# Gate and up projections in seven products of 256 tokens instead of eight

## The chip, the cores and the metric

The kernel runs on one core of a Trainium2 chip. The metric is the device time of one execution in microseconds (us). The median of three runs before the change is 852.94 us, and the three lie between 852.77 and 853.24 us. Names of the engines in the profile: PE is TensorE's matmul, PEld its weight load, DVE is VectorE, ACT is ScalarE, POOL is GpSimd, SP is SyncE, whose queue starts nearly all transfers.

## The reference

A decoder layer on 512 tokens of width 1024, all in float32:

```
proj = x @ w_in                            # q, k, v, SSM input, gate logits
y_attn = merged(dilated attention) @ w_attn_br
y_ssm  = glu(S5 scan) @ w_ssm_br
mix_out = (g0 * y_attn + g1 * y_ssm) @ w_out
h  = layer_norm(ALPHA * x + mix_out)
ff = (silu(h @ w_ff_gate) * (h @ w_ff_up)) @ w_ff_down     # 1024 -> 2816 -> 1024
x  = layer_norm(ALPHA * h + ff)
```

The change touches the last but one line alone: the products of `h` with `w_ff_gate` and `w_ff_up` (1024 by 2816 each, 22 column tiles of 128).

## The kernel before, in words

Every large product is made of three matmuls. An operand in float32 is split into a rounded part `hi` (type fp32r) and the rest `lo`, and `mm3` (lines 187 to 190) adds hi·hi, hi·lo and lo·hi into the same PSUM columns. The helper `split` (lines 179 to 185) makes the two parts: ACT copies `hi` (line 181), DVE subtracts to get `lo` (line 182).

`class Weights` streams the weights. `load` starts a transfer of one unit of 128 x 2048 floats (1 MB) on SP into one of two `raw` buffers; `split` turns half a unit (128 x 1024) into a pair `whi`, `wlo` in one of five slots (three in the early part); `release`, called in the program after the matmuls that used a slot, hands the oldest slot back and splits the next half unit. Since the order of instructions on each engine is the order in which the program issues them, these calls set the order of the work; there is no planner.

The feed-forward stage begins after the first layer norm. `turn_h` (lines 1137 to 1145) transposes 128 tokens of `h` on PE and splits the result into `hp_` (`hh`, `hl` in the profile: channels on partitions, 512 tokens along the free axis, two tiles of four 128-channel blocks each). `ff_mm(f, e, cs)` multiplies column tile `f` of the gate (`e` = 0) or up (`e` = 1) weights with the tokens `cs`: eight blocks of 128 channels, three matmuls each, 24 matmuls into one PSUM bank (`fg` in the profile). The weights are the stationary operand, the tokens stream. The first tiles run on 256 tokens at a time while the other tokens are still being transposed (lines 1202 to 1211), all others on 512. `ff_gate(f)` (lines 1187 to 1200) forms gate times sigmoid times up from the two banks with one ACT tanh and two DVE operations, and splits the result at once into `ff` hi and lo.

The down projection follows (lines 1228 to 1274): `down` uses the tokens of `ff` as the stationary operand and 512 columns of `w_ff_down` as the streaming one, into eight banks (`dn`), k-tile by k-tile. The last four k-tiles go token tile by token tile, so that the second layer norm of one token tile lies beside the matmuls of the next. `hn` holds the first layer norm's result for the residual all this time.

SBUF is managed by hand: `home(n, ...)` gives one of about a dozen 128 x 2048 areas a new name once its former content is dead, and the pool `ap_` has four more (`act`).

## Time and profile before

| what | value |
|---|---|
| median of three runs | 852.94 us |
| span of the profiled execution, first to last instruction | 851.2 us (the profile gives no other time for it; what lies around the span is 852.94 - 851.2 = 1.7 us against the median) |
| granted TensorE clock, mean | 0.998 |
| PE / PEld / DVE / ACT busy | 842.6 / 701.9 / 485.3 / 302.5 us |
| gate and up matmuls (`fg`) | 144 of 256 columns, 984 of 512 columns |
| feed-forward stage on PE | first `fg` matmul at 481.93 us, first `dn` matmul at 724.00 us |
| weight splits, all stages | 134 on ACT (1046 ns each), 134 on DVE (1227 ns each) |

Matmuls are pipelined: a matmul's listed duration contains its way through the array, and the next one starts long before it ends. Their pace is read from the distance of their starts.

### The profile page before, as it was taken

The page shows a single profiled execution, that of the slowest core. Times are in us where ns is not written, and L with a number is a line of the kernel's source. Part 1 is how long each engine was busy: PE and PEld are TensorE (multiplying, and loading weights), DVE is VectorE, ACT ScalarE, POOL GpSimd, SP SyncE. Part 2 cuts the span into 40 slices and gives each one's busy share as a digit, 9 for nine tenths or more (in the row PEclk, how much of TensorE's full clock was granted, in tenths as well). Part 3 has the DMA queues.
Part 4 walks back from the last instruction along what each step waited for, and adds up shares of the span by engine and source line. Part 5 has one row for each costly group of instructions (what it writes and reads, how often), then busy time and mean ns, then how long its engine had stood idle before and what let it go on. Part 6 is the DMA issues. An engine that isn't in the chain of part 4 may idle for free.

```text
span 851.2 us, 11299 instructions
## 1 busy us (share of the span) xinstructions
PE 842.6 (99%) x4576; PEld 701.9 (82%) x4576; DVE 485.3 (57%) x951; ACT 302.5 (36%) x481; POOL 25.5 (3%) x27
## 2 busy tenths in 40 slices
PE   9999999999999999999999999999999999999996
PEld 7888888888888888888888898888888888888886
DVE  6976899964666446347785854334344344222237
ACT  5973231264344444643241332222222222211101
POOL 0000000000000000000000500000000000000005
PEclk9999999999999999999999999999999999999999
DMA  9732421425121221121642142222222222322203
GB/s 332 185 120 89 124 99 53 146 73 176 50 99 50 102 98 52 50 91 58 248 142 105 50 149 99 99 99 99 99 100 98 89 90 88 136 98 95 99 0 100
DMA packets 23860, 90.06 MB, mean 106 GB/s; under 512 B 6272, under 2 KB 11136, under 8 KB 14464
## 3 DMA queue, kind: packets, MB, share of 16 engines
q1 hardware_dynamic: 22032, 86.59, 29.8%
q10 hardware_dynamic: 1776, 2.74, 0.9%
q8 instruction: 36, 0.59, 0.3%
q14 instruction: 16, 0.13, 0.0%
HBM read 84.87 MB, written 4.46 MB: 105 GB/s over the span
## 4 chain that ended last, share of the span: by engine, by line
PE 98%; DMA 1%; DVE 0%; ACT 0%; issue 0%; SPq 0%; DVEq 0%
PE fg L190 9%; PE fg L188 9%; PE fg L189 9%; PE dn L190 4%; PE dn L189 4%; PE dn L188 4%; PE pg L188 4%; PE pg L189 3%; PE pg L190 3%; PE pv L188 3%; PE pk L188 3%; PE pq L188 3%; PE pv L189 3%; PE pq L190 3%; PE pv L190 3%; PE pk L189 3%
## 5 line engine op out<-in xcount | busy, mean ns | idle before, releaser
L182 DVE TENSOR_TENSOR wlo<-raw,whi 128x1024 fp32r<-128x1024 f32 x134 | 164.2, 1227 | 191.3 <-ACT whi L181 191.2
L181 ACT CAST whi<-raw 128x1024 fp32r<-128x1024 f32 x134 | 140.0, 1046 | 232.8 <-PE dn L190 73.3
L188 PE MATMUL fg<-hh,whi 128*128 128x512 f32 (+1 forms) x376 | 141.3, 376 | 0.0
L189 PE MATMUL fg<-hl,whi 128*128 128x512 f32 (+1 forms) x376 | 141.2, 375 | 0.0
L190 PE MATMUL fg<-hh,wlo 128*128 128x512 f32 (+1 forms) x376 | 141.2, 375 | 0.0
L189 PEld LDWEIGHTS fg<-hl,whi 128*128 128x128 f32 x376 | 70.8, 188 | 12.9
L190 PEld LDWEIGHTS fg<-hh,wlo 128*128 128x128 f32 x376 | 70.8, 188 | 12.8
L188 PEld LDWEIGHTS fg<-hh,whi 128*128 128x128 f32 x376 | 70.8, 188 | 12.7
L188 PE MATMUL dn<-whi,ff 128*128 128x512 f32 x168 | 65.4, 389 | 0.0
L189 PE MATMUL dn<-wlo,ff 128*128 128x512 f32 x168 | 65.4, 389 | 0.0
L190 PE MATMUL dn<-whi,ff 128*128 128x512 f32 x168 | 65.4, 389 | 0.0
L188 PE MATMUL pg<-x_hi,whi 128*128 128x512 f32 x128 | 50.5, 395 | 0.0
L184 ACT ACTIVATE ff<-fth 128x512 fp32r<-128x512 f32 x22 | 14.0, 635 | 102.7 <-DVE fth L322 102.7
L190 PE MATMUL pg<-x_hi,wlo 128*128 128x512 f32 x128 | 49.9, 390 | 0.0
L189 PE MATMUL pg<-x_lo,whi 128*128 128x512 f32 x128 | 49.9, 390 | 0.0
L322 DVE TENSOR_TENSOR fth<-fth,fg 128x512 f32<-128x512 f32 x22 | 15.1, 687 | 56.9 <-PE fg L190 56.8
L188 PE MATMUL pq<-x_hi,whi 128*128 128x512 f32 x96 | 37.9, 394 | 0.0
L188 PE MATMUL pk<-x_hi,whi 128*128 128x512 f32 x96 | 37.8, 394 | 0.0
L190 PE MATMUL pq<-x_hi,wlo 128*128 128x512 f32 x96 | 37.4, 390 | 0.0
L190 PE MATMUL pk<-x_hi,wlo 128*128 128x512 f32 x96 | 37.4, 389 | 0.0
L189 PE MATMUL pk<-x_lo,whi 128*128 128x512 f32 x96 | 37.4, 389 | 0.0
L189 PE MATMUL pq<-x_lo,whi 128*128 128x512 f32 x96 | 37.4, 389 | 0.0
(257 smaller groups left out, 1458.4 us busy)
## 6 DMA issues: line engine op xcount, KB each, us to landing
raw<-in_w_in SPq DMA_DIRECT2D x26, 1024.0 KB, 4.8
raw<-in_w_gu SPq DMA_DIRECT2D x22, 1024.0 KB, 4.7
raw<-in_w_dn SPq DMA_DIRECT2D x11, 1024.0 KB, 4.7
raw<-in_w_br SPq DMA_DIRECT2D x4, 1024.0 KB, 4.7
raw<-in_w_out SPq DMA_DIRECT2D x4, 1024.0 KB, 4.7
raw_x<-in_xw SPq DMA_DIRECT2D x2, 1024.0 KB, 9.9
raw<-in_w_glu SPq DMA_DIRECT2D x2, 1024.0 KB, 4.8
xn<-in_x SPq DMA_DIRECT2D x2, 1024.0 KB, 8.0
```

The costliest lines, as they stand in the source:

```text
L181: act.copy(hi, src)
L182: dve.tensor_tensor(lo, src, hi.bitcast(F32), op=ALU.subtract)
L184: act.mul(hi, src, scale)
L188: pe.matmul(dst, a[0], b[0], start=first, stop=False)
L189: pe.matmul(dst, a[0], b[1], start=False, stop=False)
L190: pe.matmul(dst, a[1], b[0], start=False, stop=last)
L322: eng.tensor_tensor(o, a, b, op=op)
```

## The change

Column tiles 0 and 1 stay as they are (`NPLAIN` = 2). The other 20 tiles are taken in ten pairs. For a pair, the weights are seen as four blocks: a11 and a12 are tile 2j (gate and up) with the first and the last four channel blocks, a21 and a22 the same of tile 2j+1; `h` is four blocks too, by channel half and by token half. Strassen's scheme (with Winograd's sums) then needs seven products of blocks where the plain way needs eight. One product is 24 matmuls of 256 columns: two column tiles (gate, up), four channel blocks, three matmuls.

- **Sums of `h`**, once: four DVE operations of 128 x 1024 on a float32 copy `ht` of the transposed `h`, then three splits (`t23` of 2048 columns, `t4` and `t1` of 1024). `turn_h` writes that copy with one more ACT operation per 512 columns.
- **Sums of weights**, for each pair: four DVE operations of 128 x 1024 into `sums`. A pair has seven split operands (three plain blocks, four sums) where it had four. A split's DVE half (`lo`) is put off to the next call of `flush`.
- **Products** for pair j in the order 2, 5, 6, 3, 7, (1 of the next pair), 4, with three banks per pair, which alternate. Bank x takes 1, 6, 7, 4 one upon the other, bank z takes 5 and 3, bank y takes 2. Between two products into one bank its state is read out (`evict`): ACT copies 1, 5, 6 and 4; DVE adds in after 2, 3 and 7. After product 4 ACT makes one tanh of 1024 columns, and DVE finishes the pair with two operations of 1024 columns (`finish_pair`), placed ahead of the read-out of the next product 2.
- **ff** is kept in float32 and split in the down stage (`ff_split`, 11 times 128 x 1024), two of these already beside the last products.
- **hn** is written to DRAM in four transfers (0.5 MB each) at the start of the stage, since its areas take `ff`, and is read back in two (1 MB each) at the start of the down stage.

The weights' bytes are the same; their layout in DRAM is prepared on the host so that each half unit is one block.

```diff
 N_BR = N_GLU + 4
 N_OUT = N_BR + 8
 N_FF = N_OUT + 8
-N_DOWN = N_FF + 2 * NFF
+NPLAIN = 2
+N_DOWN = N_FF + 2 * NPLAIN
 NLAST = 4
 
...
+        if self.first_loads and 2 * m == self.first_job:
+            self.first_loads.popleft()()
             return
...
+        if self.jobs and n == self.first_job:
+            self.jobs.popleft()()
+            return
+        self.flush()
...
+    def flush(self):
+        if self.after:
+            self.after()
+            self.after = None
...
-    for f in range(NFF):
+    for f in range(NPLAIN):
         w.add(i["w_gu"][f], 8)
+    w.first_job = 2 * len(w.units)
...
+    NPR = NFF // 2
+    ra, rb = {}, {}
+
+    def load_a(j):
+        if j < NPR:
+            ra[j] = wp.tile([P, 2048], F32, tag="wraw", name=f"ra{j}", bufs=2)
+            sp.dma_start(ra[j], i["w_gu"][2 * j])
+        else:
+            w.load()
+
+    def load_b(j):
+        if j < NPR:
+            rb[j] = home(("g0", 2)[j % 2], f"rb{j}")
+            sp.dma_start(rb[j], i["w_gu"][2 * j + 1])
+
+    w.first_loads.extend((lambda j=j: load_a(j)) for j in (1, 2))
...
-            split(hp_[0][j][:, :, tsl], hp_[1][j][:, :, tsl], b.rearrange("p (e c) -> p e c", e=4))
+            bv = b.rearrange("p (e c) -> p e c", e=4)
+            full = ht[t // 2][:, 4 * j : 4 * j + 4, 128 * (t % 2) : 128 * (t % 2) + 128]
+            act.copy(full, bv)
+            act.copy(hp_[0][j][:, :, tsl], bv)
+            tt(hp_[1][j][:, :, tsl], full, hp_[0][j][:, :, tsl].bitcast(F32), ALU.subtract)
...
+    FF_HOMES = ("act", "g2", 0, "g3", 4, 5)
+    ffs = {}
+
+    def ff_at(f, n):
+        if f // 4 not in ffs:
+            h = FF_HOMES[f // 4]
+            z = ap_.tile([P, 2048], F32, tag="act", name=f"ff{f // 4}") if h == "act" else home(h, f"ff{f // 4}")
+            ffs[f // 4] = z.rearrange("p (f t) -> p f t", f=4)
+        return ffs[f // 4][:, f % 4 : f % 4 + n, :]
...
-        tt(th, th, fb[f, 1], ALU.mult)
-        split(cur[:, 0, f % 2, :], cur[:, 1, f % 2, :], th, 0.5)
+        tt(ff_at(f, 1)[:, 0, :], th, fb[f, 1], ALU.mult)
...
+    sums = home(6, "sums").rearrange("p (n c) -> p n c", n=2)
+    quad = home(3, "quad").rearrange("p (c e t) -> p c e t", c=4, e=2)
+    ops = {}
+    for j in (1, 2):
+        load_b(j)
+
+    def prepare(j, n):
+        hi, lo = w.take_slot(f"{j}{n}")
+        ops[j, n] = tuple(z.rearrange("p (e k c) -> p e k c", e=2, k=4) for z in (hi, lo))
+        a11, a12 = (ra[j][:, 1024 * e : 1024 * e + 1024] for e in range(2))
+        a21, a22 = (rb[j][:, 1024 * e : 1024 * e + 1024] for e in range(2))
+        s0, s1 = sums[:, 0], sums[:, 1]
+        src = {1: a11, 2: a12, 4: a22, 5: s0, 6: s1, 3: s0, 7: s1}[n]
+        if n == 5:
+            tt(s0, a21, a22, ALU.add)
+        elif n == 6:
+            tt(s1, s0, a11, ALU.subtract)
+        elif n == 3:
+            tt(s0, a12, s1, ALU.subtract)
+        elif n == 7:
+            tt(s1, a11, a21, ALU.subtract)
+        act.copy(hi, src)
+        w.flush()
+
+        def rest():
+            tt(lo, src, hi.bitcast(F32), ALU.subtract)
+            if n == 7:
+                load_a(j + 2)
+            elif n == 4:
+                load_b(j + 2)
+
+        w.after = rest
+
+    order = [(1, 1)]
+    for j in range(1, NPR):
+        order += [(j, 2), (j, 5), (j, 6), (j, 3), (j, 7)] + [(j + 1, 1)] * (j + 1 < NPR) + [(j, 4)]
+    w.jobs.extend((lambda j=j, n=n: prepare(j, n)) for j, n in order)
+
+    psb = {}
+
+    def product(j, n):
+        x, y, z = ((4, 5, 6), (1, 0, 7))[(j - 1) % 2]
+        b = {1: x, 2: y, 5: z}.get(n)
+        key = {1: "x", 6: "x", 7: "x", 4: "x", 2: "y", 5: "z", 3: "z"}[n]
+        if b is not None:
+            psb[j, key] = bank(b, f"fs{j}{key}")
+        d = psb[j, key]
+        wh, wl = ops.pop((j, n))
+        mh, ml = forms[n]
+        for e in range(2):
+            for k in range(4):
+                c = d[:, 256 * e : 256 * e + 256]
+                for m, (p_, q_) in enumerate(((wh, mh), (wh, ml), (wl, mh))):
+                    pe.matmul(c, p_[:, e, k, :], q_[:, k, :], start=(b is not None and e == k == m == 0),
+                              stop=(k == 3 and m == 2), skip_group_check=True)
+
+    snap = {}
+
+    def taken(name, j):
+        snap[name] = bt.tile([P, 512], F32, tag=f"snap{name}", name=f"snap{name}{j}", bufs=1)
+        return snap[name]
+
+    def quarter(c):
+        return quad[:, c].rearrange("p e t -> p (e t)")
+
+    def finish_pair(j):
+        th, gate, up = snap["th"], quad[:, :, 0, :], quad[:, :, 1, :]
+        stt(th, th, 1.0, gate, ALU.add, ALU.mult)
+        tt(ff_at(2 * j, 2).rearrange("p f (h t) -> p (f h) t", h=2), th, up, ALU.mult)
+
+    def evict(j, n):
+        if n == 1:
+            act.copy(taken("1", j), psb[j, "x"])
+        elif n == 2:
+            if j > 1:
+                finish_pair(j - 1)
+            tt(quarter(0), snap["1"], psb[j, "y"], ALU.add)
+        elif n == 5:
+            act.copy(taken("5", j), psb[j, "z"])
+        elif n == 6:
+            act.copy(taken("6", j), psb[j, "x"])
+        elif n == 3:
+            tt(quarter(1), snap["6"], psb[j, "z"], ALU.add)
+        elif n == 7:
+            tt(quarter(3), snap["5"], psb[j, "x"], ALU.add)
+        else:
+            act.copy(quarter(2), psb[j, "x"])
+            snap["th"] = bt.tile([P, 1024], F32, tag="fth", name=f"fth{j}s", bufs=1).rearrange("p (c t) -> p c t", c=4)
+            act.activation(snap["th"], quad[:, :, 0, :], AF.Tanh, scale=0.5)
...
+    for t in range(NTT):
+        sp.dma_start(hdr[:, t, :], hn[t])
+
+
+    h1, h2 = ht
+    tt(h1[:, 0:4], h2[:, 0:4], h1[:, 0:4], ALU.subtract)
+    tt(h2[:, 0:4], h2[:, 4:8], h2[:, 0:4], ALU.subtract)
+    tt(h2[:, 4:8], h2[:, 4:8], h1[:, 0:4], ALU.subtract)
+    tt(h1[:, 4:8], h1[:, 4:8], h2[:, 4:8], ALU.subtract)
+    t23 = [ap_.tile([P, KT, 256], F32R, tag="act", name=f"t23{n}") for n in "hl"]
+    t4 = ap_.tile([P, 2, 4, 256], F32R, tag="act", name="t4")
+    t1 = [hp_[n][0][:, :, 256:512] for n in range(2)]
+    forms = {1: [hp_[n][0][:, :, 0:256] for n in range(2)], 2: [hp_[n][1][:, :, 0:256] for n in range(2)],
+             3: [hp_[n][1][:, :, 256:512] for n in range(2)], 4: [t4[:, n] for n in range(2)], 5: t1,
+             6: [t23[n][:, 4:8] for n in range(2)], 7: [t23[n][:, 0:4] for n in range(2)]}
...
+        if n == 0:
+            split(t23[0], t23[1], h2)
+        elif n == 1:
+            split(t4[:, 0], t4[:, 1], h1[:, 4:8])
...
-    for f in range(2, NFF):
-        for e in range(2):
-            ff_mm(f, e, slice(0, 512))
-            w.release()
-        ff_gate(f)
...
+    split(t1[0], t1[1], h1[:, 0:4])
+
+    ffhl = {}
+    SPLIT_HOMES = ((7, "g1"), (8, 1), ("act", "act"), ("act", 6), ("act", "g2"), (0, "g3"))
...
+        fs = slice(2 * (jj % 2), 2 * (jj % 2) + 2)
+        split(ffhl[s_][0][:, fs, :], ffhl[s_][1][:, fs, :], ffs[s_][:, fs, :], 0.5)
+
+    for j, n in order:
+        product(j, n)
+        evict(j, n)
+        w.release()
+        if j == NPR - 1 and n in (3, 7):
+            ff_split((0, 1)[n == 7])
...
+    finish_pair(NPR - 1)
+
+    hns = []
+    for j, h in enumerate(("g0", 2)):
+        hns.append(home(h, f"hr{j}").rearrange("p (t d) -> p t d", t=2))
+        sp.dma_start(hns[j], hdr[:, 2 * j : 2 * j + 2, :])
...
+        if k % 2 == 0:
+            ff_split(k // 2 + 2)
...
+    gu = pairs(gu, 8, P).reshape(NFF, P, 2, 2, 512)
+    gu = np.concatenate([gu[:NPLAIN], gu[NPLAIN:].transpose(0, 1, 3, 2, 4)]).reshape(NFF, P, 2048)
```

Three places of the order, each before and after. The line numbers after the change are those of the changed kernel.

PE where one group of 24 matmuls ends and the next begins (`fg`, `fs` are PSUM banks; `hh`, `hl`, `t23h`, `t23l` operands from `h`). Before, within the plain tiles:

```order
L188 MATMUL fg_4813<-hh_3888,whi_91_4705 128x512
L189 MATMUL fg_4813<-hl_3890,whi_91_4705 128x512
L190 MATMUL fg_4813<-hh_3888,wlo_91_4706 128x512
L188 MATMUL fg_4850<-hh_3887,whi_92_4742 128x512 [waits Activation_49]
L189 MATMUL fg_4850<-hl_3889,whi_92_4742 128x512
L190 MATMUL fg_4850<-hh_3887,wlo_92_4743 128x512 [waits DVE_49]
```

After, from product 5 to product 6 of pair 3 (bank z to bank x):

```order
L1296 MATMUL fs3z<-hh_3887,whi_35_4881 128x256
L1296 MATMUL fs3z<-hl_3889,whi_35_4881 128x256
L1296 MATMUL fs3z<-hh_3887,wlo_35_4882 128x256
L1296 MATMUL fs3x<-t23h,whi_36_4913 128x256 [waits Activation_49]
L1296 MATMUL fs3x<-t23l,whi_36_4913 128x256
L1296 MATMUL fs3x<-t23h,wlo_36_4914 128x256 [waits DVE_49]
```

The groups still have 24 matmuls and wait at their start for the two halves of a split; the matmuls have 256 columns, and the group writes into a bank that holds an earlier product.

DVE over one pair of column tiles in the middle of the stage (`wlo` is the second half of a split, `fth` and `ff` the gating). Before, the whole of it:

```order
L182 TENSOR_TENSOR wlo_102_5076<-raw_4975,whi_102_5075 128x1024 [waits DMAHW5_49,Activation_49]
L182 TENSOR_TENSOR wlo_103_5105<-raw_4975,whi_103_5104 128x1024 [waits PE_49,Activation_49]
L319 SCALAR_TENSOR_TENSOR fth_5110<-fth_5110,fg_5050 128x512 [waits Activation_49]
L322 TENSOR_TENSOR fth_5110<-fth_5110,fg_5079 128x512 [waits DVE_49,PE_49]
L185 SCALAR_TENSOR_TENSOR ff_5043<-fth_5110,ff_5043 128x512 [waits Activation_49]
L182 TENSOR_TENSOR wlo_104_5142<-raw_5041,whi_104_5141 128x1024 [waits DMAHW6_49,Activation_49]
L182 TENSOR_TENSOR wlo_105_5171<-raw_5041,whi_105_5170 128x1024 [waits PE_49,Activation_49]
L319 SCALAR_TENSOR_TENSOR fth_5177<-fth_5177,fg_5116 128x512 [waits Activation_49]
L322 TENSOR_TENSOR fth_5177<-fth_5177,fg_5145 128x512 [waits DVE_49,PE_49]
L185 SCALAR_TENSOR_TENSOR ff_5176<-fth_5177,ff_5176 128x512 [waits Activation_49]
```

After, 12 of the 16 rows of a pair: `sums` are weight sums, `quad` the read-outs with a sum, `fth2s` the end of the pair before:

```order
L337 TENSOR_TENSOR sums<-rb_4633 128x1024 [waits DMAHW3_49,DVE_49]
L337 TENSOR_TENSOR wlo_32_4851<-ra_4572,whi_32_4850 128x1024 [waits Activation_49]
L337 TENSOR_TENSOR sums<-sums,ra_4572 128x1024 [waits DVE_49]
L337 TENSOR_TENSOR wlo_35_4882<-sums,whi_35_4881 128x1024 [waits Activation_49]
L337 TENSOR_TENSOR sums<-ra_4572,sums 128x1024 [waits DVE_49]
L337 TENSOR_TENSOR wlo_36_4914<-sums,whi_36_4913 128x1024 [waits Activation_49]
L334 SCALAR_TENSOR_TENSOR fth2s<-fth2s,quad 128x1024 [waits Activation_49]
L337 TENSOR_TENSOR ff_4976<-fth2s,quad 128x1024 [waits DVE_49]
L337 TENSOR_TENSOR quad<-snap_4911,fs3y 128x512 [waits DVE_49,PE_49]
L337 TENSOR_TENSOR sums<-ra_4572,rb_4633 128x1024
L337 TENSOR_TENSOR wlo_33_4946<-sums,whi_33_4945 128x1024 [waits Activation_49]
L337 TENSOR_TENSOR wlo_37_4980<-sums,whi_37_4979 128x1024 [waits Activation_49]
```

The pair had ten DVE operations and has 16, 13 of them of 1024 columns. The weight sums stand ahead of the subtractions that need them, and the end of pair 2 stands between the sums of pair 3.

ACT over the same stretch (`whi` is the first half of a split). Before, for two column tiles:

```order
L181 CAST whi_88_4609<-raw_4509 128x1024 [waits DMAHW6_49,PE_49]
L181 CAST whi_89_4638<-raw_4509 128x1024 [waits PE_49,Activation_49]
L1197 ACTIVATE fth_4645<-fg_4584 128x512 [waits PE_49,Activation_49]
L184 ACTIVATE ff_4644<-fth_4645 128x512 [waits DVE_49]
L181 CAST whi_90_4676<-raw_4576 128x1024 [waits DMAHW7_49,PE_49]
L181 CAST whi_91_4705<-raw_4576 128x1024 [waits PE_49,Activation_49]
L1197 ACTIVATE fth_4711<-fg_4651 128x512 [waits PE_49,Activation_49]
L184 ACTIVATE ff_4644<-fth_4711 128x512 [waits DVE_49]
```

After, all 12 rows of a pair (`snap` are read-outs without a sum, `quad<-fs2x` that of product 4):

```order
L1264 CAST whi_35_4881<-sums 128x1024 [waits DVE_49,PE_49,Activation_49]
L1315 COPY snap_4911<-fs3x 128x512 [waits PE_49]
L1264 CAST whi_36_4913<-sums 128x1024 [waits DVE_49,Activation_49]
L1329 COPY quad<-fs2x 128x512 [waits PE_49]
L1331 ACTIVATE fth2s<-quad 128x1024 [waits Activation_49]
L1264 CAST whi_33_4945<-sums 128x1024 [waits DVE_49]
L1264 CAST whi_37_4979<-sums 128x1024 [waits DVE_49]
L1321 COPY snap_5009<-fs3z 128x512 [waits PE_49]
L1264 CAST whi_41_5011<-ra_4793 128x1024 [waits DMAHW4_49]
L1323 COPY snap_5041<-fs3x 128x512 [waits PE_49]
L1264 CAST whi_34_5043<-rb_4633 128x1024 [waits DMAHW3_49]
L1264 CAST whi_42_5072<-ra_4793 128x1024
```

Each read-out now stands between two copies for the splits, and copies that take a weight sum wait for DVE.

33 lines of the change are left out of this document (18 added, 15 removed).

## The prediction

> **What bounds the kernel now.** I read the page first (busy times, then the chain of waits), then the groups by shape, then the start times on PE. The page's head, its busy row and the engines in its chain:
>
> ```profile
> span 851.2 us, 11299 instructions
> PE 842.6 (99%) x4576; PEld 701.9 (82%) x4576; DVE 485.3 (57%) x951; ACT 302.5 (36%) x481; POOL 25.5 (3%) x27
> PE 98%; DMA 1%; DVE 0%; ACT 0%; issue 0%; SPq 0%; DVEq 0%
> ```
>
> PE is busy for 99% of the span and makes 98% of the chain. Whatever shortens PE's stream shortens the kernel, as long as DVE (57%) and ACT (36%) keep up. The groups by shape that this change touches (mean ns of one after the comma):
>
> ```profile
> L188 PE MATMUL fg<-hh,whi 128*128 128x512 f32 x328 | 127.6, 389 | 0.0
> L188 PE MATMUL fg<-hh,whi 128*128 128x256 f32 x48 | 13.7, 284 | 0.0
> L182 DVE TENSOR_TENSOR wlo<-raw,whi 128x1024 fp32r<-128x1024 f32 x134 | 164.2, 1227 | 191.3 <-ACT whi L181 191.2
> L181 ACT CAST whi<-raw 128x1024 fp32r<-128x1024 f32 x134 | 140.0, 1046 | 232.8 <-PE dn L190 73.3
> L322 DVE TENSOR_TENSOR fth<-fth,fg 128x512 f32<-128x512 f32 x22 | 15.1, 687 | 56.9 <-PE fg L190 56.8
> L1197 ACT ACTIVATE fth<-fg 128x512 f32<-128x512 f32 x22 | 13.0, 593 | 0.0
> L764 ACT COPY v<-pv 128x512 f32<-128x512 f32 x12 | 7.1, 589 | 7.5 <-PE pv L190 7.2
> ```
>
> A matmul's listed time (389 ns for 512 columns, 284 for 256) holds its way through the array. The pace is the distance of starts, from the timeline of PE:
>
> ```profile
> 489.55 0.28 PE L189 MATMUL fg<-hl,whi 128*128 128x256 f32 x1
> ...
> 500.82 0.28 PE L190 MATMUL fg<-hh,wlo 128*128 128x256 f32 x1
> 500.94 0.40 PE L188 MATMUL fg<-hh,whi 128*128 128x512 f32 x1
> ...
> 723.78 0.39 PE L190 MATMUL fg<-hh,wlo 128*128 128x512 f32 x1
> 724.00 0.39 PE L188 MATMUL dn<-whi,ff 128*128 128x512 f32 x1
> ```
>
> From 489.55 to 500.82 us 94 matmuls of 256 columns start after one another: 11.27 / 94 = 0.1199 us. From 500.94 to 723.78 us it is 983 of 512 columns (984 = 3 x 328, less the first): 222.84 / 983 = 0.2267 us. So half the columns cost 53%, not 50%: about 13 ns of each matmul do not scale. The pace is not idle time in disguise, and it holds beside busy neighbours, as the windows say (columns: length, then busy time and count of PE, PEld, DVE, ACT, POOL, granted clock):
>
> ```profile
> 484.50:487.50 3.00, 3.00 (x27) 3.00 (x27) 3.00 (x4) 0.00 (x0) 1.81 (x2) 1.00 0.00 0
> 489.60:500.80 11.20, 11.20 (x95) 11.20 (x95) 6.34 (x10) 4.84 (x7) 0.00 (x0) 1.00 0.46 154
> 502.00:724.00 222.00, 222.00 (x981) 183.81 (x980) 90.37 (x102) 63.07 (x82) 0.00 (x0) 1.00 0.28 98
> 724.00:835.00 111.00, 111.00 (x491) 91.93 (x490) 32.58 (x38) 20.31 (x20) 3.64 (x4) 1.00 0.24 82
> ```
>
> In the first window DVE is busy all the time, and 27 matmuls (some two of them cut by its edges) still take 3.00 us. In the 256-column stretch the weight load is busy all the time as well (11.20 of 11.20), against 184 of 222 us among the 512-column ones.
>
> **The PE term.** A pair of column tiles had 2 x 2 x 24 = 96 matmuls of 512 columns, 96 x 0.2267 = 21.76 us. It gets 7 x 24 = 168 of 256 columns, 168 x 0.1199 = 20.14 us; one product is 2.88 us. Ten pairs: 217.6 - 201.4 = 16.2 us saved. Seven eighths of the arithmetic would have been 27.2 us; the 13 ns on 720 more matmuls take the rest. The point of no gain is a pace of 960 x 0.2267 / 1680 = 0.1295 us.
>
> The Trainium skill (TensorE: Matmul & The Clock Gate, "Back-to-back issue gap") gives sustained paces for pairs of weight load and matmul of about 81 ns at 128 columns and 131 ns at 512. By a straight line between these, 256 columns cost three quarters of 512, and the stage would be estimated some 66 us longer; the trace's 0.1199 against 0.2267 us does not agree with it.
>
> **The supply of a pair.** DVE gets 7 subtractions, 4 weight sums and 2 closing operations of 1024 columns, all of the form of the `wlo` row (1.23 us), and 3 read-outs of 512 (0.69 us): 13 x 1.23 + 3 x 0.69 = 18.1 of 20.14 us. Before it was 4 x 1.23 + 6 x 0.69 = 9.1 of 21.76. ACT gets 7 copies of 1024 (1.05 us), 4 read-outs of 512 (0.59) and a tanh of 1024, which I put at 1.05: 10.8 us. Neither is over PE's time, so what matters is who waits for whom. The handshakes:
>
> ```profile
> 599.99 1.23 DVE L182 TENSOR_TENSOR wlo<-raw,whi 128x1024 fp32r<-128x1024 f32 x1 [2.79 <-ACT whi L181]
> 601.14 0.68 DVE L319 SCALAR_TENSOR_TENSOR fth<-fth,fg 128x512 f32<-128x512 f32 x1
> 604.10 0.39 PE L190 MATMUL fg<-hh,wlo 128*128 128x512 f32 x1
> 604.53 0.69 DVE L322 TENSOR_TENSOR fth<-fth,fg 128x512 f32<-128x512 f32 x1 [2.71 <-PE fg L190]
> 605.25 0.64 ACT L184 ACTIVATE ff<-fth 128x512 fp32r<-128x512 f32 x1 [4.79 <-DVE fth L322]
> 605.91 0.69 DVE L185 SCALAR_TENSOR_TENSOR ff<-fth,ff 128x512 fp32r<-128x512 f32 x1 [0.70 <-ACT ff L184]
> 609.79 1.05 ACT L181 CAST whi<-raw 128x1024 fp32r<-128x1024 f32 x1 [2.98 <-PE fg L189]
> 610.75 0.59 ACT L1197 ACTIVATE fth<-fg 128x512 f32<-128x512 f32 x1
> 150.57 0.68 DVE L322 TENSOR_TENSOR swk<-swk,rope 128x512 f32<-128x512 f32 x1
> 151.28 1.08 DVE L322 TENSOR_TENSOR k<-cqk,swk 128x512 f32<-128x512 f32 x1
> ```
>
> An independent DVE operation starts 0.08 us before its forerunner's listed end (599.99 + 1.23 against 601.14), one on ACT 0.09 us before; a dependent one 0.03 us after it (150.57 to 151.28, likewise 604.53 + 0.69 to 605.25 across engines). DVE begins 0.43 us after the start of the last matmul that it waits for; with 256 columns (0.11 us shorter), that is 0.20 us after the next group could start. The independent starts make DVE's pair 11 x 1.15 + 2 x 1.26 + 3 x 0.61, some 17.0 us.
>
> The longest chain inside a pair runs from the end of product 4 to the start of the next product 3, which writes into bank z and so needs product 5's read-out. It is: 0.20 to ACT, read-out of 4 0.59, tanh 1.05, two closing operations on DVE 1.23 each, read-out after product 2 0.61, weight sum for 7 1.23, its copy on ACT 0.96, read-out of 5 0.59, and six gaps of 0.03: 7.9 us. DVE comes in time for the closing: from the end of product 7 it needs 0.2 + 0.61 + 6 x 1.15 = 7.7 us for one read-out, three sums and three subtractions, and the tanh is there after 2 x 2.88 + 0.2 + 0.59 + 1.05 and gaps, 7.7 us too. PE works meanwhile on products 2, 5 and 6, 3 x 2.88 = 8.6 us. So 0.7 us is left, and PE does not stop. The other operands have more: each is split three products ahead, and by the same steps the subtraction for product 3 is done about 1.2 us before its use, that for product 7 about 2.8 us. With that cover, the sums, splits and read-outs cost nothing.
>
> The unknown sizes in that chain are the tanh of 1024 columns and the two closing operations, whose operands are every other 256 columns of `quad`. From below they cost as above. From above stand rows that move 1024 and 512 columns in a scattered order, the cast below and the 1.08 us of 151.28:
>
> ```profile
> L487 ACT CAST xt<-x_lo 128x1024 fp32r<-128x1024 f32 x4 | 8.3, 2070 | 0.0
> ```
>
> By 2.07 us for the tanh and 1.08 / 0.69 of the price for the two on DVE the chain is 7.9 + 1.0 + 1.4 = 10.3 us, 1.7 us too long in each pair. I take the lower end: runs of 256 columns in order are nearer to the plain rows.
>
> **The start of the stage.** Here the sums of `h` come in.
>
> ```profile
> 487.69 1.91 PE L1144 MATMUL hb<-ident,hn 128*128 128x128 f32 x16
> 488.32 2.05 ACT L181 CAST hh<-hb 128x512 fp32r<-128x512 f32 x4 [4.78 <-PE hb L1144]
> 488.95 2.47 DVE L182 TENSOR_TENSOR hl<-hb,hh 128x512 fp32r<-128x512 f32 x4
> raw<-in_w_gu SPq DMA_DIRECT2D x22, 1024.0 KB, 4.7
> xn<-in_x SPq DMA_DIRECT2D x2, 1024.0 KB, 8.0
> ```
>
> The last four `hh` copies took ACT from 488.32 us on, 0.51 us each; now there are eight, to 492.4, and the last `hl` is done at 493.1. The 256-column group on the first tokens lasts until 489.55 + 23 x 0.12 = 492.3, and the next group needs the later blocks only 1.4 us in, so that is covered. The like copies for tokens 128 to 255 lie just ahead of the norm of the last token tile; I give 0.5 us to its delay. DVE goes on: four sums of `h`, each waiting for the last (1.26), to 498.1; ACT's 2048-column copy for `t23` to 498.9; then on DVE 2.3 (`t23`), 1.15 (product 1 had its copy long ago), 1.15 (`t4`), 1.3 (gate 0), 4 x 1.15 (sums and subtractions for 2, 5, 6), to 509.4; gate 1 waits for its tanh to 509.9 and takes 1.3; `t1` 1.23: 512.5. PE gets to product 5, which needs `t1`'s second half, at 500.94 + 24 x 0.2267 + 2 x 2.88 = 512.1. So 0.3 us, and about 0.2 behind it. Together 1.0 us, once. Below, 0; above, what the transfers add: the second weight buffer, both b blocks and four writes of `hn` (5 MB) stand one behind the other on SP from about 489 us, when DVE has done the split ahead of `hl`. One transfer lands after 4.7 us, two together after 8.0; at 3.3 us more for each MB the first b block lands at 489 + 8.0 to 11.3, in time for the sum at 504.8, but at 507 if all 5 MB share the way, which adds 2.2 us.
>
> **The down stage.** Nine of the eleven deferred splits come here, 9 x 1.23 = 11 us more on DVE, which was busy for 32.58 of 111 us, and 9.5 on ACT (20.31). The first is placed two products ahead of its use. Without that cover the bound is one split, 2.3 us, once. `hn` comes back 18 k-tiles before its use (18 x 24 x 0.2267 = 98 us). The gating of the last pair is needed at k-tile 20. Cost nothing.
>
> **Sum.** 851.2 - 16.2 + 1.0 = 836.0 us of span, with 1.7 us around it 837.7 us; the median shown is 1.7 us above the span, so the sum is the same against it.
>
> **Rivals.**
> 1. *PE sets the pace, small loss at the start* (forecast): 837.7, from 836.7 (no loss) to 839.9 (shared transfers). Chance 0.70.
> 2. *The chain through tanh and closing is too long*, and PE stops before product 3 once per pair. For it: only 0.7 us of slack, some of its operations are in no row. Against: 10.3 us needs scattered rows. At 0.7 us a pair (halfway) 837.7 + 7 = 845. Chance 0.17.
> 3. *DVE becomes the bound.* Its queue is in order, each subtraction waits for ACT, and ACT's copy may stand behind a read-out that waits for PE. Idle time already occurs there:
>
> ```profile
> DVE wlo L182 <- ACT whi L181: 191.2, 92, 8.6
> ```
>
>    The mean is 191.2 / 92 = 2.08 us. Two such waits a pair make 18.1 + 4.2 = 22.3 us, 0.5 us over the old pair: 852.9 + 1.0 + 5 = 859. It decides from 2 us of DVE waiting a pair, and the kernel is slower from 3.7. Against: those waits were ACT standing for PE to free a slot, with DVE early; the copies now come three products ahead. Chance 0.11.
> 4. *The weight load doesn't keep up* and a matmul of 256 columns costs more than 0.1295 us. The load is always busy there, at 188 ns listed; were these strung up, 1680 x 0.188 = 315.8 us against 217.6, and the time 951. The stretch of 94 speaks against any such thing. Chance 0.02. It is the direction of the sustained paces that the Trainium skill's page on TensorE (named above) states.
>
> **How the numbers follow.** About 0.2% (1.7 us) can be told from no change. Faster: case 1 and most of 2, 0.86. Slower: case 3 without its mild end, 4 and the far end of 2, 0.11. Within 0.2%: 0.03. The range takes case 1 with its bounds and case 2 to a little over 1 us a pair: 836 to 849; outside stay case 3, 4 and the tail of 2, under 0.2.
>
> **What would show it.** Right: 1680 matmuls `fs` starting every 0.120 us, a product every 2.88 us, pairs every 20.1 us, DVE some 85 to 90% busy in the stage, PE without idle time but for about 1 us between 505 and 520 us. Case 2: PE waiting before product 3 for ACT's `snap` of 5. Case 3: PE waiting for `wlo` again and again, pairs of 21 us and more, DVE without gaps. Transfers: DVE waiting for `rb` at 505 us. The prediction is wrong if the pairs do not come every 20.1 us, or if the matmuls `dn` come more slowly than every 0.2267 us.

## The result, and the profile after

| what | before | after |
|---|---|---|
| median of the runs timed together | 853.09 us (852.77 to 853.62, 4 runs) | 838.37 us (838.32 to 838.9, 4 runs) |
| ratio, 95% interval | | 0.9828 [0.9814, 0.9842] |
| span of the profiled execution | 851.2 us | 836.9 us |
| granted clock, mean | 0.998 | 0.998 |

The kernel became faster by 14.7 us; the forecast of 837.7 us is 0.7 us below the median. The profiled execution is the longest of the four (838.9 us); the spans of the other three are 836.4 to 836.5 us. The page of the changed kernel: span, busy row, engines in the chain of waits.

```profile
span 836.9 us, 12834 instructions
PE 827.2 (99%) x5296; PEld 723.7 (86%) x5296; DVE 589.8 (70%) x1027; ACT 357.5 (43%) x541; POOL 25.8 (3%) x27
PE 98%; DVE 1%; DMA 1%; issue 0%; ACT 0%; SPq 0%; DVEq 0%
```

PE still makes 98% of the chain, with 720 matmuls more and 15.4 us less of busy time. DVE has gained 104.5 us and ACT 55 us; DVE has 1% of the chain, ACT nothing. Window by window (same columns as in the prediction), the middle of the stage, then most of the down stage:

```profile
600.00:700.00 100.00, 100.00 (x836) 100.00 (x835) 85.25 (x80) 49.56 (x59) 0.00 (x0) 1.00 0.27 92
709.00:820.00 111.00, 111.00 (x494) 92.08 (x493) 44.27 (x45) 30.89 (x31) 3.57 (x3) 1.00 0.29 107
```

In the first, 836 matmuls in 100 us without a moment of idle time on PE, the weight load always busy too, DVE at 85%. In the second PE is as full as before, and DVE has 44.3 instead of 32.6 us.

**Where the 14.3 us of span come from.** Start times on PE, after, at the four borders of the stage; the table puts those of before beside them (its rows are in the prediction; the first `fg` there is at 481.93 us). The row behind them is from before: the first matmul of tile 2, the 25th of 512 columns.

```profile
482.26 0.28 PE L202 MATMUL fg<-hh,whi 128*128 128x256 f32 x1
...
506.90 0.28 PE L1296 MATMUL fs1x<-hh,whi 128*128 128x256 f32 x1
...
709.62 0.40 PE L202 MATMUL dn<-whi,ffh 128*128 128x512 f32 x1
```

```profile
506.41 0.39 PE L188 MATMUL fg<-hh,whi 128*128 128x512 f32 x1
```

| stretch | before | after | change | forecast |
|---|---|---|---|---|
| all ahead of the first `fg` | 481.93 | 482.26 | +0.33 | +0.5 |
| first `fg` to the first product (tiles 0 and 1) | 24.48 | 24.64 | +0.16 | 0 |
| the 20 tiles | 217.59 | 202.72 | -14.87 | -16.2 + 0.5 |
| first `dn` to the end | 127.2 | 127.3 | +0.1 | 0 |
| sum | | | -14.3 | -15.2 |

In the 20 tiles, a product comes every 2.88 us (in pair 5 at 590.50, 593.38, 596.26, 599.14, 602.02, 604.90 and 607.78 us), which is 0.1200 us a matmul: 1680 x 0.1200 = 201.6 us. The other 1.1 us are two stops. One, 0.1 us, is at product 5 of pair 1, where it was forecast. The other wasn't forecast. It is in pair 10, the last, and the timeline of PE shows it:

```profile
705.46 0.28 PE L1296 MATMUL fs10x<-t23l,whi 128*128 128x256 f32 x1
705.58 0.28 PE L1296 MATMUL fs10x<-t23h,wlo 128*128 128x256 f32 x1
706.64 0.51 PE L1296 MATMUL fs10x<-t,whi 128*128 128x256 f32 x2 [0.78 <-DVE quad L337]
706.98 0.28 PE L1296 MATMUL fs10x<-t,wlo 128*128 128x256 f32 x1
```

From 705.58 to 706.64 us is 1.06 us where 0.12 is the pace: 0.94 us lost, and another 0.10 at the second matmul behind it (the two of the third row and their follower take 706.98 - 706.64 = 0.34 instead of 0.24). The row names DVE's read-out `quad`. The timeline of DVE at that moment:

```profile
704.76 1.22 DVE L199 SCALAR_TENSOR_TENSOR ffl<-ff,ffh 128x1024 fp32r<-128x1024 f32 x1
705.89 0.69 DVE L337 TENSOR_TENSOR quad<-snap,fs10x 128x512 f32<-128x512 f32 x1
```

Product 7 and product 4 both go into bank x, and between them DVE has to read out the bank. In pairs 1 to 9 product 1 of the next pair stands between the two and gives DVE 2.88 us. The last pair has no next one: product 4 follows product 7 at once, and PE stands for the handshake and the whole read-out (0.20 us + 0.69 us and the way back).

**The chain that the forecast put at 0.7 us from deciding** can be read for pair 5 (end of product 4 of pair 4, 590.50 us, to product 3). On ACT and on DVE:

```profile
590.70 0.59 ACT L1329 COPY quad<-fs4x 128x512 f32<-128x512 f32 x1 [0.53 <-PE fs4x L1296]
591.32 1.06 ACT L1331 ACTIVATE fth4s<-quad 128x1024 f32<-128x1024 f32 x1
...
596.92 1.05 ACT L1264 CAST whi<-sums 128x1024 fp32r<-128x1024 f32 x1 [3.60 <-DVE sums L337]
597.87 0.58 ACT L1321 COPY snap<-fs5z 128x512 f32<-128x512 f32 x1
```

```profile
592.48 1.22 DVE L334 SCALAR_TENSOR_TENSOR fth4s<-fth4s,quad 128x1024 f32<-128x1024 f32 x1
593.73 1.22 DVE L337 TENSOR_TENSOR ff<-fth4s,quad 128x1024 f32<-128x1024 f32 x1
595.06 0.69 DVE L337 TENSOR_TENSOR quad<-snap,fs5y 128x512 f32<-128x512 f32 x1
595.66 1.22 DVE L337 TENSOR_TENSOR sums<-ra,rb 128x1024 f32<-128x1024 f32 x1
```

The tanh of 1024 columns takes 1.06 us (put at 1.05), the two closing operations 1.22 us each: the rows that were missing before lie at the plain price, not the scattered one. The chain ends with `snap` of product 5 at 597.87 + 0.58 = 598.45 us, and PE gets to product 3 at 599.14 us. That leaves 0.69 us, less a handshake.

### The profile page after: what moved, and what is told of

It is laid out like the page before. It is cut to its first block, busy times and chain, and to the rows that moved or that the text cites. A ratio compares the mean times of both kernels' runs of the same rounds, so it can differ in the third digit from the quotient of the medians.

```text
span 836.9 us, 12834 instructions
## 1 busy us (share of the span) xinstructions
PE 827.2 (99%) x5296; PEld 723.7 (86%) x5296; DVE 589.8 (70%) x1027; ACT 357.5 (43%) x541; POOL 25.8 (3%) x27
## 4 chain that ended last, share of the span: by engine, by line
PE 98%; DVE 1%; DMA 1%; issue 0%; ACT 0%; SPq 0%; DVEq 0%
PE dn L203 5%; PE dn L202 5%; PE dn L204 5%; PE pg L202 4%; PE pg L204 3%; PE pg L203 3%; PE pv L202 3%; PE pk L202 3%; PE pq L202 3%; PE pv L203 3%; PE pq L204 3%; PE pv L204 3%; PE pk L204 3%; PE pq L203 3%; PE pk L203 3%; PE pu L602 2%
## 5 line engine op out<-in xcount | busy, mean ns | idle before, releaser
L196 DVE TENSOR_TENSOR wlo<-raw,whi 128x1024 fp32r<-128x1024 f32 x94 | 115.1, 1227 | 117.2 <-ACT whi L195 117.2
L195 ACT CAST whi<-raw 128x1024 fp32r<-128x1024 f32 x94 | 98.2, 1048 | 160.6 <-PE dn L204 63.5
L1264 ACT CAST whi<-sums 128x1024 fp32r<-128x1024 f32 x40 | 42.0, 1050 | 95.6 <-DVE sums L337 95.6
L202 PE MATMUL dn<-whi,ffh 128*128 128x512 f32 x168 | 65.4, 389 | 0.0
L203 PE MATMUL dn<-wlo,ffh 128*128 128x512 f32 x168 | 65.4, 389 | 0.0
L204 PE MATMUL dn<-whi,ffl 128*128 128x512 f32 x168 | 65.4, 389 | 0.0
L337 DVE TENSOR_TENSOR wlo<-sums,whi 128x1024 fp32r<-128x1024 f32 x40 | 48.7, 1220 | 0.0
L202 PEld LDWEIGHTS dn<-whi,ffh 128*128 128x128 f32 x168 | 31.6, 188 | 6.6
L204 PEld LDWEIGHTS dn<-whi,ffl 128*128 128x128 f32 x168 | 31.5, 188 | 6.6
L203 PEld LDWEIGHTS dn<-wlo,ffh 128*128 128x128 f32 x168 | 31.6, 188 | 6.4
```

Source lines behind the costliest of these rows:

```text
L195: act.copy(hi, src)
L196: dve.tensor_tensor(lo, src, hi.bitcast(F32), op=ALU.subtract)
L202: pe.matmul(dst, a[0], b[0], start=first, stop=False)
L203: pe.matmul(dst, a[0], b[1], start=False, stop=False)
L204: pe.matmul(dst, a[1], b[0], start=False, stop=last)
L337: eng.tensor_tensor(o, a, b, op=op)
```

## The experiments

Names of the medians: "before" is the old kernel's in the same set, 852.92 to 853.28 us. Where no range is given, there was one execution.

### Half the columns, without the scheme

The old kernel, its tiles 2 to 21 in two halves of 256 tokens: 1920 matmuls of 256 columns instead of 960 of 512, with the same weights, splits and gating. It measures the per-matmul price alone.

```diff
-            ff_mm(f, e, slice(0, 512))
+            for c0 in range(0, 512, 256):
+                ff_mm(f, e, slice(c0, c0 + 256))
```

> The kernel before, with the gate and up matmuls of tiles 2 to 21 in two halves of 256 columns and nothing else changed: no scheme, no sums. If PE's pace alone makes the price (0.1199 us for 256 columns, 0.2267 for 512), 1920 x 0.1199 - 960 x 0.2267 = 12.6 us are added: 865.5 us, and the scheme's eighth of 230 us (28.8 us) less these 12.6 is the 16.2 us of the prediction. If the small loss of the change (16.2 forecast on PE, 14.7 seen) sits in a pace that is worse in long stretches, it is 867 or more. If the weight load can't keep up over long stretches (rival 4), it is above 870.

Measured: 865.79 us (865.66 to 866.28), ratio 1.015 [1.0133, 1.0167], 12.7 us more. Where only 94 matmuls in a row carried the pace of 0.1199 us before, now 1920 do, and they give 12.7 / 1920 = 6.6 ns over half of 0.2267 us, a pace of 0.1200 us. So in the changed kernel halving the width costs about 11 us (1680 x 6.6 ns), and the eighth saved, 27.2 us, less this is the gain of 16. The rival in which the weight load falls behind is out; the straight line through the sustained paces that the Trainium skill gives (named in the prediction) is out with it.

### A quarter of the columns

```diff
-            ff_mm(f, e, slice(0, 512))
+            for c0 in range(0, 512, 128):
+                ff_mm(f, e, slice(c0, c0 + 128))
```

> The same in quarters of 128 columns, to see what the 13 ns that do not scale are. If they are a fixed cost of each matmul, 128 columns cost 0.0533 + 0.0135 = 0.067 us: 3840 x 0.067 = 257 us for the 20 tiles, 40 us more than before, about 893 us. If the weight load sets a floor near the 0.115 us that the 192-column matmuls at the end of the kernel show, it is 3840 x 0.115 = 442 us, 224 us more, about 1077 us.

Measured: 1064.35 us, span 1062.6 us. PE in the middle of the stage, and the window around it:

```profile
559.77 0.28 PE L188 MATMUL fg<-hh,whi 128*128 128x128 f32 x1
...
560.88 0.28 PE L189 MATMUL fg<-hl,whi 128*128 128x128 f32 x1
```

```profile
520.00:620.00 100.00, 100.00 (x898) 100.00 (x897) 20.58 (x24) 14.04 (x18) 0.00 (x0) 1.00 0.16 54
```

Ten matmuls in 1.11 us; over all 3840, (217.6 + 1062.6 - 851.2) / 3840 = 0.1117 us each. A fixed part added to a price per column would have put 128 columns well below that: by the steps from 512 to 256 it is 0.1200 - 0.1067 = 0.013 us and 0.417 ns a column, 0.067 us for 128. So there is a floor near 0.112 us for a weight load with its matmul, and 256 columns lie just above it. The last matmuls of the kernel before (`dq`) fit: those of 320 columns come every 0.147 us (841.12 to 842.88 us, 12 steps), which is on that line; those of 192 every 0.110 us (842.88 to 844.09 us, 11 steps; the expectation had 0.115), where the line gives 0.093. In the window the weight load is always busy while DVE and ACT have little to do. That the weight load is what sets the floor is argued from this and not tested: in the stretches of 256 columns it is always busy as well. The scheme's next level, products of 128 tokens, would have 49/64 x 3840 = 2940 matmuls, an estimated 2940 x 0.1117 = 328 us where one level takes 201.6.

### The changed kernel without the weight sums

```diff
-        src = {1: a11, 2: a12, 4: a22, 5: s0, 6: s1, 3: s0, 7: s1}[n]
-        if n == 5:
-            tt(s0, a21, a22, ALU.add)
...
+        src = {1: a11, 2: a12, 4: a22, 5: a22, 6: a11, 3: a12, 7: a21}[n]
```

> The changed kernel without the 40 weight sums on VectorE: the products that need a sum take a plain block in its place (the gate and up results are wrong by that). DVE has 4.6 us less of some 17.3 us in each pair of 20.1. If PE sets the pace and the sums are hidden (forecast), the time stays within 0.5 us of the changed kernel's 838.4 (at most the stalls of 0.1 us at the start go). If DVE is what the pairs wait for (rival 3), it falls by several us.

The kernel leaves out the 40 sums; the products that need one take a plain block in its place. Measured: 838.29 us (838.23 to 838.93), ratio to before 0.9828 [0.9814, 0.9843]: the time of the change with its sums. The window of the middle of the stage:

```profile
600.00:700.00 100.00, 100.00 (x836) 100.00 (x835) 63.22 (x60) 49.83 (x60) 0.00 (x0) 1.00 0.27 92
```

DVE falls from 85 to 63 us in 100, and PE has its 836 matmuls as before. The 40 sums are free where they stand. The stop in the last pair stays (0.94 us, from 705.10 to 706.16 us), so the sums aren't its cause either; the 0.1 us at product 5 of pair 1 is gone.

### Two extra operations on DVE in each pair, then eight

Additions of 512 columns into an area that nobody reads, half of them ahead of the read-out of product 3, half ahead of that of 7; the `pad` loop has `range(1)` and `range(4)`.

```diff
         elif n == 3:
+            for _ in range(4):
+                tt(pad, sums[:, 0, 0:512], sums[:, 1, 0:512], ALU.add)
             tt(quarter(1), snap["6"], psb[j, "z"], ALU.add)
...
```

> The changed kernel with two more DVE additions of 128x512 in each pair, off the chain (ahead of the read-outs after products 3 and 7, where DVE waits for PE for 1.6 and 1.0 us). DVE goes from 17.3 to some 18.7 us of 20.14 in each pair. If PE sets the pace, the time stays at 838.4 within 0.5 us; if DVE is near its limit already (rival 3), 5 us and more are added.

Measured with two: 839.41 us, 1.0 us more. In pairs 1 to 9 PE doesn't stop for it. The whole of it is at the stop that was there already (1.96 us lost where it was 0.94):

```profile
705.03 0.28 PE L1297 MATMUL fs10x<-t23h,wlo 128*128 128x256 f32 x1
707.11 0.39 PE L1297 MATMUL fs10x<-t,whi 128*128 128x256 f32 x1 [1.79 <-DVE quad L337]
```

> The same with eight such additions: 17.3 + 8 x 0.7 = 22.9 us of DVE work for a pair of 20.14 us. DVE must now be the bound: 2.7 us more a pair, about 838 + 27 = 865 us, slower than the kernel before. This gives the point from which rival 3 decides.

Measured with eight: 871.97 us, slower than before and 7 us over the expectation. The window and two of the stops:

```profile
600.00:700.00 100.00, 90.89 (x743) 89.39 (x743) 97.48 (x104) 43.29 (x52) 0.00 (x0) 1.00 0.25 85
```

```profile
618.70 0.28 PE L1297 MATMUL fs6x<-hh,wlo 128*128 128x256 f32 x1
620.28 0.36 PE L1297 MATMUL fs5x<-t,whi 128*128 128x256 f32 x1 [1.30 <-DVE quad L337]
...
631.75 0.28 PE L1297 MATMUL fs6x<-t23h,wlo 128*128 128x256 f32 x1
633.01 0.39 PE L1297 MATMUL fs6z<-hh,whi 128*128 128x256 f32 x1 [0.98 <-ACT snap L1322]
```

PE stops twice in a pair: 1.46 us before product 4, which waits for DVE's late read-out of 7, and 1.15 + 0.1 us before product 3, where ACT's read-out of 5 is late because the weight sum ahead of it is. A pair takes 22.9 us (631.75 - 608.81, the same place one pair earlier, is 22.94) instead of 20.16. DVE is busy for 97.5%: now it is the bound. So the rival with DVE as the bound is a true mechanism that does not act here. Four additions keep DVE from 612.15 us to the next row at 614.93, so eight take 2 x 2.78 = 5.6 us of its time a pair, and they cost 2.8; some 2.8 us a pair can be used up before the time moves in every pair.

The pairs came as expected (20.16 + 2.8 us); what was not expected is the last one:

```profile
730.42 0.28 PE L1297 MATMUL fs10x<-t23h,wlo 128*128 128x256 f32 x1
737.35 0.58 PE L1297 MATMUL fs10x<-t,whi 128*128 128x256 f32 x1 [6.65 <-DVE quad L337]
```

There product 4 follows 7 at once, and the read-out of 7 stands on DVE behind the eight additions and the first deferred split, so that PE loses 6.81 us where the changed kernel lost 0.94. After that the granted clock is 0.51 for 5.8 us (737.3 to 743.1 us), which costs 2.3 us up to the first `dn`. The nine other pairs cost 25.0 us: 25.0 + 5.9 + 2.3 = 33.2 us, the difference of the two spans (870.1 and 836.9).

### Another order in the last pair

In pair 10, 5, 6, 2, 7, 3, 4 instead of 2, 5, 6, 3, 7, 4, so that 7 and 4 no longer stand together; the sum for product 3 is made one step later.

```diff
-        elif n == 3:
+        elif n == 3 and j < NPR - 1:
             tt(s0, a12, s1, ALU.subtract)
         elif n == 7:
+            if j == NPR - 1:
+                tt(s0, a12, s1, ALU.subtract)
             tt(s1, a11, a21, ALU.subtract)
...
-    for j in range(1, NPR):
+    for j in range(1, NPR - 1):
...
+    order += [(NPR - 1, n) for n in (5, 6, 2, 7, 3, 4)]
```

> The changed kernel with the products of the last pair in the order 5, 6, 2, 7, 3, 4 instead of 2, 5, 6, 3, 7, 4, so that no product follows at once upon another in the same bank; everything is computed. In the trace of the change PE stood 0.94 us before product 4 of pair 10, which there follows product 7 in bank x without the next pair's product 1 between. If this is its cause, the span falls by 0.9 us to 836.0 and the time to 837.5. If it is only the visible end of a lag of DVE, the wait moves to another product and the time stays.

Measured: 837.41 us (837.33 to 837.78), ratio to before 0.9817 [0.9802, 0.9832]; span 835.4. The place on PE:

```profile
705.12 0.28 PE L1299 MATMUL fs10z<-hh,wlo 128*128 128x256 f32 x1
705.24 0.40 PE L1299 MATMUL fs10x<-t,whi 128*128 128x256 f32 x2
...
708.12 0.40 PE L202 MATMUL dn<-whi,ffh 128*128 128x512 f32 x1
```

Product 4 starts 0.12 us after the last matmul of 3: the stop is gone and with it its cause is settled. From the first product to the first `dn` it is 201.66 us (506.46 to 708.12) against 202.72: 1.06 us, the 0.94 and the 0.10 behind it. The rest of the 1.5 us between the two spans lies ahead of the stage, where the two kernels do the same. This version beats both kernels.

### The new order with two extra operations on DVE

> e7_dve2 (two more DVE additions of 128x512 per pair) with the order of e4_last for the last pair. In e7_dve2 1.96 us of PE's idle time stood before product 4 of pair 10 and none in the other pairs. If DVE's spare time in the pairs is free and the 1.0 us that e7 cost came through that one place, the time is that of e4_last, 837.4 within 0.3 us. If the additions cost something in each pair, it is above 838.

The edit is that of the run with two additions, on the kernel with the new order. Measured: 838.48 us (838.23 to 839.0), ratio to before 0.9828 [0.9811, 0.9844], 1.1 us over the new order alone (against different executions of before, 853.28 and 853.06). That was not expected: with the stop in pair 10 gone, I held the two operations to be free. PE at the start of the down stage:

```profile
708.64 0.40 PE L203 MATMUL dn<-wlo,ffh 128*128 128x512 f32 x1
709.93 0.50 PE L204 MATMUL dn<-whi,ffl 128*128 128x512 f32 x1 [0.89 <-DVE ffl L199]
```

No pair stops, but the third matmul `dn` waits 1.06 us for `ffl`, the first of the deferred splits, and the timeline of DVE says when that is made:

```profile
706.92 0.68 DVE L337 TENSOR_TENSOR quad<-snap,fs10z 128x512 f32<-128x512 f32 x1
707.52 1.22 DVE L196 TENSOR_TENSOR wlo<-raw,whi 128x1024 fp32r<-128x1024 f32 x1
708.65 1.22 DVE L199 SCALAR_TENSOR_TENSOR ffl<-ff,ffh 128x1024 fp32r<-128x1024 f32 x1
```

It stands behind the read-out of product 3 and ends at 709.87 us. The code puts split 0 behind product 3 and split 1 behind product 7. In the changed kernel 3 comes first; in the new order 7 does, so that split 0, which is needed first, had moved from two products ahead of its use to one. A side effect of my own edit, then, or a lack of DVE time at the end of the stage whatever the order. One more run tells the two apart.

### The same, with the two deferred splits in their old order

```diff
-            ff_split((0, 1)[n == 7])
+            ff_split((1, 0)[n == 7])
```

> The new order in the last pair with two extra additions on DVE per pair, and the two deferred splits that stand beside the last products change places, so that the first one (read by the first matmuls of the down stage) is again two products ahead of its use, as it is in the changed kernel; the new order alone, which ends with 7, 3, 4, had put it behind product 3, one product ahead. Theory A: the 1.06 us stop at the third matmul dn came from this place of the first split. Then the stop is gone, the two additions are free, and the time is that of the new order alone, 837.4 to 837.9 us. Rival B: the end of the stage is short of DVE time whatever the order of the two splits. Then a stop of about 1 us stays, at the start of the down stage or at the matmuls that need the second split (four rows of 24 matmuls later), and the time is 838.5 us.

Measured: 837.27 us (837.04 to 837.59), ratio to before 0.9816 [0.98, 0.9832]. PE at the same place:

```profile
708.45 0.39 PE L203 MATMUL dn<-wlo,ffh 128*128 128x512 f32 x1
708.68 0.40 PE L204 MATMUL dn<-whi,ffl 128*128 128x512 f32 x1
```

The stop is gone, and two more operations on DVE in every pair cost nothing that can be measured. It was the place of the split. Without the two additions this order of products and splits is the one to keep; it was not run in that form.

### The tanh twice, three times, four times

The line is repeated, which lengthens the chain from product 4 to product 3 by one, two and three steps of 1.09 us (the starts of the repeated tanhs on ACT lie 1.09 to 1.10 us apart), and changes nothing else.

```diff
             act.activation(snap["th"], quad[:, :, 0, :], AF.Tanh, scale=0.5)
+            act.activation(snap["th"], quad[:, :, 0, :], AF.Tanh, scale=0.5)
```

> The changed kernel with each pair's tanh done twice (1.06 + 0.03 us more on ACT in the chain from the end of product 4 to the start of the next product 3). The slack in the trace of the change is 0.66 us in pair 5 (read-out of product 5 done at 598.45 us, product 3 at 599.14). If the chain of the prediction is right, PE stops 0.4 us before product 3 in each of the nine pairs that have a pair before them: 838.4 + 3.9 = 842. If the slack is much larger than forecast, nothing happens; if PE already waits there, 9 x 1.09 = 9.8 us are added: 848.

Measured with two: 843.25 us (843.04 to 843.65), ratio to before 0.9883 [0.9867, 0.99]. PE before product 3 of pair 5:

```profile
600.71 0.28 PE L1296 MATMUL fs5x<-t23h,wlo 128*128 128x256 f32 x1
601.23 0.39 PE L1296 MATMUL fs5z<-hh,whi 128*128 128x256 f32 x1 [0.23 <-ACT snap L1321]
601.45 0.28 PE L1296 MATMUL fs5z<-hl,whi 128*128 128x256 f32 x1
```

0.52 us where 0.12 is the pace, so 0.40 us lost, waiting for `snap` of 5, and so in each of nine pairs (0.39 to 0.40). The slack of 0.66 us read in the trace of the change had given 0.43, the prediction's 0.7 us gives 0.39. It is a direct measurement of the slack: 1.09 - 0.40 = 0.69 us. The 0.10 us at the next matmul (0.22 instead of 0.12) I had not counted; 9 x 0.50 is 4.5 us, and the last pair adds 0.3, since its read-out of 7 is later too (1.25 us lost instead of 0.94).

> The changed kernel with each pair's tanh done three times, between e5_tanh1 and e6_tanh3: 2.1 us more in the chain, so PE should stand 1.48 us before product 3 in nine pairs, with 0.1 us for starting again, and 0.6 us more at the last pair than in the changed kernel: 838.4 + 9 x 1.58 + 0.6 = 853.2. In e6_tanh3 PE stood 2.57 us and then mostly ran for 3.4 us at a granted clock of 0.51, which cost 13 us beyond the expectation. If such a fall needs a longer stop than 1.5 us, the time is 853; if it comes with any stop, about 1.6 us more a pair: 867.

Measured with three: 853.06 us. The stop is 1.48 to 1.49 us in each of nine pairs, one step longer, and 0.10 behind it.

> The same with the tanh done four times: 3.2 us more in the chain. Past the slack every us must count once per pair: 9 x (3.2 - 0.66) = 23 us, about 861 us; pairs of 22.7 us. If another path has taken over by then, more.

Measured with four, ahead of the run with three: 874.58 us, span 872.8, where 861 was expected. The stops are as foreseen, 2.57 to 2.58 us nine times. But the mean granted clock is 0.983, and the windows of a stop and of what follows it (pair 2, then pair 8) say why:

```profile
538.90:541.40 2.50, 0.18 (x2) 0.00 (x0) 2.50 (x3) 1.48 (x3) 0.00 (x0) 1.00 0.17 26
543.05:546.50 3.45, 3.45 (x19) 3.45 (x18) 1.21 (x3) 1.72 (x2) 0.00 (x0) 0.51 0.28 114
684.50:687.00 2.50, 0.20 (x2) 0.00 (x0) 2.50 (x3) 1.46 (x3) 0.00 (x0) 1.00 0.35 52
687.20:708.00 20.80, 20.33 (x168) 20.13 (x168) 15.22 (x15) 11.56 (x13) 0.00 (x0) 1.00 0.25 94
```

After the stop of pair 2 there are 3.45 us at a clock of 0.51, with 19 matmuls (those cut by the window's edges included) where 29 belong: in it a matmul starts every 0.213 us, 16 times, which loses 16 x 0.093 = 1.5 us. After that of pair 8 there is none of this, and the pair takes 22.83 us (start of the stop to the next, 684.42 to 707.25) instead of some 24.3 like the others. Eight of nine stops have it. 836.9 + 9 x 2.67 + 8 x 1.5 = 872.9 us, which is the span.

### The copies ahead of the norm

The kernel with the new order, and in `turn_h` both splits are made from the PSUM bank first; the float32 copies of `h` come behind them.

```diff
+        fulls = []
...
-            act.copy(full, bv)
-            act.copy(hp_[0][j][:, :, tsl], bv)
-            tt(hp_[1][j][:, :, tsl], full, hp_[0][j][:, :, tsl].bitcast(F32), ALU.subtract)
+            split(hp_[0][j][:, :, tsl], hp_[1][j][:, :, tsl], bv)
+            fulls.append((full, bv))
+        for full, bv in fulls:
+            act.copy(full, bv)
```

> The order of e4_last, and in turn_h both splits straight from the transposed h first, the float32 copies behind them (the four ACT copies of a token tile in another order, everything computed). In the trace of the change the first gate matmul comes 0.33 us later than before and the first product 0.52 us later than before's group at that place (506.90 against 506.38 us). If the copies ahead of the last norm are the cause, as the prediction had it, some 0.3 to 0.5 us come back against e4_last: 837.0. If it is not these copies, the time stays at 837.4.

Measured: 837.8 us (837.22 to 837.9), ratio to before 0.9818 [0.9804, 0.9833]; the new order alone had 0.9817. No difference that can be measured in the time. The trace shows a small one:

```profile
481.93 0.28 PE L202 MATMUL fg<-hh,whi 128*128 128x256 f32 x1
...
506.40 0.28 PE L1301 MATMUL fs1x<-hh,whi 128*128 128x256 f32 x1
```

24.47 us for tiles 0 and 1, as before the change (24.48); with the copies ahead it was 24.64 in the changed kernel and in the new order alone (481.82 to 506.46). So the copies cost 0.17 us, and behind the first `fg`, not ahead of it.

## Why the prediction was right, and where it was not

**What bounds the kernel, and the PE term: right.** PE's stream set the time before and sets it after. The term was 16.2 us; from starts it is 217.6 - 1680 x 0.1200 = 16.0. The run with halves shows the price per matmul over a whole stage, without the scheme. The rival in which the weight load does not keep up is out.

**The supply of a pair: right, by its own margin.** Product 3 would wait if the chain were 0.7 us longer, the prediction said. It starts 0.69 us after the last read-out that it needs, and lengthening the chain by one, two and three steps gives stops of 0.40, 1.48 and 2.57 us. The rival with the long chain needed scattered prices for the tanh and the closing operations; they cost 1.06 and 1.22 us. The one with DVE as the bound put the turning point at 2 us a pair, which came from prices without the overlap of independent operations (18.1 us a pair); with it the prediction had 17.0 us, measured are 17.2 (85.25 us in 100), and some 2.8 us can be used up. Without the sums nothing gets faster.

**The start of the stage: too dear.** The term was 1.0 us: 0.5 for the copies ahead of the last norm, 0.3 at product 5 and 0.2 behind it. The runs show 0.3: 0.16 us in tiles 0 and 1 and 0.1 at product 5. That step failed on its first part. The first `fg` is indeed 0.33 us later, but that isn't the copies: the transposes of `h` ahead of it (`hb`) start at 473.32 us before and at 473.64 after, and from there to the first `fg` it is 8.61 us and 8.62. At the first `gl` (369.38 and 369.71 us), where both kernels still do the same, the difference is there in full. In other executions with the copies in the same place the first `fg` comes at 481.71 us (two extra operations on DVE) to 482.55 us (tanh four times). It is scatter between executions. The transfers, the upper bound of that part, were in time: the first sum that reads `rb` starts on DVE without a wait, where 504.8 us was forecast:

```profile
504.33 0.69 DVE L337 TENSOR_TENSOR ff<-fth,fg 128x512 f32<-128x512 f32 x1
504.94 1.22 DVE L337 TENSOR_TENSOR sums<-rb 128x1024 f32<-128x1024 f32 x1
```

**The step that was missing: the last pair.** The supply was worked out for a pair in the middle, with product 1 of the next pair between 7 and 4. The list of products in the code says that this product exists only while there is a next pair. I did not follow it to its end, and it cost 0.94 + 0.10 us; the other order takes it away. It offset the 0.7 us too much at the start, which is why the sum (836.0 us of span against 836.9) is nearer than its terms; that much of the agreement is luck.

**The down stage: right.** From the first to the last matmul it is as long as before. The first deferred split was said to be covered by two products, and the runs with two additions show what the cover is worth: with two products ahead PE does not stop, with one it stops for 1.06 us.

**Around the span** 1.7 us were assumed; in the four executions it is 1.8 to 2.0 us (838.9 with a span of 836.9, 838.32 with 836.4, 838.41 and 838.33 with 836.5). The shorter three lie 0.4 to 0.5 us above the 836.0 us of the forecast.

## What to carry to other kernels

Price a matmul by the distance of starts at its own width, in a stretch of the trace that is full, and set a scheme that saves arithmetic by narrower pieces against that price: here an eighth less work gave 16 of 27 us, and the next level, by the estimate above, would lose. When work is hidden behind a pipelined loop, work out the longest chain in the order in which the engines get it, and do it again for the first and the last turn, where the neighbour that covers a read-out is missing. Terms that offset each other make a sum look better than its steps; compare the stretches, not the total.
